# v and the attention values as two 1024-column groups with seven block products

## The chip, the cores and the metric

One core of one Trainium2 chip. The metric is the device time of one execution in microseconds; the kernel before takes 1322.12 us, the median of three runs (1322.08 to 1322.16).

## What is computed

One layer of an encoder on 256 tokens of width 2048, in float32, and a final norm. The parts that the change touches:

```
h = RMSNorm(x);  P = h @ w_in            # columns [u, v | q, k, values | gates]
v = LayerNorm(gelu(v));  y_A = u' * (W_s @ v + b)            # u' = gelu(u), 8 groups
y_B = neighbourhood attention of q, k and the values, 16 heads
m = sigmoid(g_A) * (y_A @ Wb_A) + sigmoid(g_B) * (y_B @ Wb_B)
x = x + m @ w_out;  then a gated convolutional MLP, and the final RMSNorm
```

The scale of the first norm is taken out of the product: the matmuls run on x times the norm's weight, and each row's factor comes in when the product is read.

## The kernel before

Every operand of a product is split into a high part, rounded by ScalarE to the type that TensorE takes in one pass (`whi`, L143), and the rest, a subtraction on VectorE (`wlo`, L144). A product is then three matmuls: high by high, low by high, high by low.

The weights come in **pieces** of 512 KB, numbered through the whole program, in the order in which the groups were planned. `begin(i)` (L168) is what is issued ahead of the matmuls of piece i: loads up to piece i + 4 on SP's queue, roundings up to piece i + 3 (one piece ahead in the first four), and the tasks that were set for i with `at(i, f)`, in the order in which they were set. From piece 5 on the roundings stand ahead of the tasks, before it behind them. Each engine works in the order of issue. Five load buffers and four pairs of rounded buffers turn round: a load waits until VectorE has read the piece five before, a rounding until TensorE has used the piece four before.

Three kinds of group use the pieces. `natural` (L181) takes 512 columns, two 128-row blocks of the weights a piece, the activations held still: 12 matmuls a piece. `stationary` (L185) holds the weights still. `wide` (L260, `run_wide` L324) takes 1024 columns, one 128-row block a piece, 12 matmuls as well. For the tile pairs in `quads` it forms seven block products in place of eight from sums of the tiles: 9 matmuls in the first piece of the pair, 12 in the second. For that VectorE makes sums of the weights three pieces ahead (`weight_sums` L305), which are split two pieces ahead (`weight_sums_split` L314), and sums of the activations (`act_sums` L287, `act_sums_split` L298). The products that belong to several outputs have four banks of their own, which are added up and read after the last pair; with the four of the group that is all eight banks.

x is transposed in eight chunks of two 128-column blocks (`x_chunk` L491: four transposes, two ScalarE and two VectorE operations). Piece 0 begins when x and the first weights are there; chunk c is turned at piece c - 1 and its load stands on SP's queue among those of the weights. The squares of x are summed in pieces 5 to 8 and the norm is made in piece 9 (`x_norm` L1126).

The order of the groups before: v as two natural groups (pieces 0 to 15, evicted by ScalarE with gelu), u as two stationary ones, then values, q and k, gates and branch products in turns (`g_at` L1075), the second halves of the gates as two wide groups (`g_gw` L1086, pairs 1, 3, 5), and from there branch products, w_out, the MLP. The values are copied to window tiles by POOL's queue (L618). The attention of a pair of heads runs as tasks beside the pieces (`attend` L710); the merged values are transposed as tasks two pieces after their group (`turn_m` L852).

## Time and profile before

| | us |
|---|---|
| median of three runs | 1322.12 |
| profiled execution | 1321.89 |
| its span | 1319.9 |
| TensorE busy | 1307.3 |
| VectorE busy | 1030.5 |
| ScalarE busy | 755.0 |

The span is the time from the first to the last instruction of the profiled execution. Busy times overlap. A matmul is shown from its start to a modelled end, so that neighbours overlap too; what one costs is the distance between starts. An operation of VectorE or ScalarE is shown slightly longer than the distance to the next one behind it.

### The profile page before, as it was taken

The numbers are of one execution on the slowest core, as the hardware profiler recorded it, in microseconds if no ns is written. First come the engines' busy times: TensorE is split into PE (matmuls) and PEld (weight loads), VectorE is DVE, ScalarE is ACT, GpSimd is POOL, SyncE is SP. The second block draws the span as 40 slices with busy tenths as digits, with TensorE's granted clock in tenths as the row PEclk, the third lists the DMA queues.
The fourth block names the chain that finished last, engine by engine and source line by source line (L and its number), as shares of the span: only waits on it lengthen the run. The fifth ranks groups of instructions, "written<-read, shape, count | busy, mean of one in ns | idle before, by whom it ended". The sixth has DMA issues, their size and how long they took to land.

```text
span 1319.9 us, 19273 instructions
## 1 busy us (share of the span) xinstructions
PE 1307.3 (99%) x6791; PEld 1115.5 (85%) x6791; DVE 1030.5 (78%) x1561; ACT 755.0 (57%) x1127; POOL 101.6 (8%) x192
## 2 busy tenths in 40 slices
PE   9999999999999999999999999999999999999997
PEld 7888888888887888888888888888888888888885
DVE  6477667767598966996787878787878779999997
ACT  6565566667554644556655556565555556555653
POOL 0241155530000000000000000000000000000000
PEclk9999999999999999999999999999999999999999
DMA  9766775755666666665656665656566657656663
GB/s 317 231 189 183 216 224 165 218 173 155 199 176 208 200 197 221 219 214 162 191 179 195 184 194 181 202 176 204 180 195 187 192 154 229 220 192 206 212 197 122
DMA packets 174800, 259.37 MB, mean 197 GB/s; under 512 B 12920, under 2 KB 124400, under 8 KB 174704
## 3 DMA queue, kind: packets, MB, share of 16 engines
q1 hardware_dynamic: 170416, 250.31, 60.9%
q0 software_dynamic: 3968, 7.30, 2.2%
q8 instruction: 53, 0.87, 0.3%
q10 hardware_dynamic: 320, 0.53, 0.1%
q14 instruction: 43, 0.35, 0.1%
HBM read 253.90 MB, written 2.10 MB: 194 GB/s over the span
## 4 chain that ended last, share of the span: by engine, by line
PE 98%; DVE 1%; DMA 0%; ACT 0%; issue 0%; SPq 0%; ACTq 0%; DVEq 0%
PE bank L196 31%; PE bank L200 16%; PE bank L285 10%; PE bank L283 10%; PE bank L284 10%; PE bank L224 7%; PE bank L226 7%; PE bank L225 7%; PE bank L722 1%; DMA wraw<-in_w_in_dram 0%; PE bank L772 0%; PE bank L598 0%; PE bank L762 0%; PE bank L933 0%; PE bank L496 0%
## 5 line engine op out<-in xcount | busy, mean ns | idle before, releaser
L144 DVE TENSOR_TENSOR wlo<-wraw,whi 128x1024 fp32r<-128x1024 f32 (+1 forms) x471 | 553.6, 1186 | 225.6 <-ACT whi L143 120.9
L143 ACT ACTIVATE whi<-wraw 128x1024 fp32r<-128x1024 f32 (+1 forms) x471 | 475.3, 1022 | 225.9 <-PE bank L225 72.1
L196 PE MATMUL bank<-h,whi 128*128 128x512 f32 x1760 | 425.2, 392 | 0.0
L196 PEld LDWEIGHTS bank<-h,whi 128*128 128x128 f32 x1760 | 322.5, 189 | 61.6
L200 PEld LDWEIGHTS bank<-h,wlo 128*128 128x128 f32 x1760 | 225.9, 191 | 8.8
L200 PE MATMUL bank<-h,wlo 128*128 128x256 f32 x1760 | 228.6, 283 | 0.0
L958 ACT ACTIVATE tc<-ta,ck 128x256 f32<-128x256 f32 x86 | 47.1, 594 | 117.1 <-DVE ta L956 117.1
L224 PE MATMUL bank<-whi,h 128*128 128x512 f32 x256 | 102.4, 400 | 0.6 <-ACT whi L143 0.6
L285 PE MATMUL bank<-wlo,a 128*128 128x512 f32 x260 | 101.6, 391 | 0.2 <-DVE wlo L144 0.2
L283 PE MATMUL bank<-whi,a 128*128 128x512 f32 x260 | 101.3, 390 | 0.0
L284 PE MATMUL bank<-whi,a 128*128 128x512 f32 x260 | 101.3, 390 | 0.0
L225 PE MATMUL bank<-whi,h 128*128 128x512 f32 x256 | 100.1, 391 | 0.3 <-DVE h L475 0.3
L226 PE MATMUL bank<-wlo,h 128*128 128x512 f32 x256 | 100.2, 391 | 0.0
L285 PEld LDWEIGHTS bank<-wlo,a 128*128 128x128 f32 x260 | 48.8, 188 | 11.3 <-DVE wlo L144 1.3
L284 PEld LDWEIGHTS bank<-whi,a 128*128 128x128 f32 x260 | 48.9, 188 | 10.1
L283 PEld LDWEIGHTS bank<-whi,a 128*128 128x128 f32 x260 | 48.8, 188 | 10.1
L224 PEld LDWEIGHTS bank<-whi,h 128*128 128x128 f32 x256 | 48.3, 189 | 10.4 <-ACT whi L143 1.1
L226 PEld LDWEIGHTS bank<-wlo,h 128*128 128x128 f32 x256 | 48.1, 188 | 10.6 <-DVE wlo L144 0.4
L225 PEld LDWEIGHTS bank<-whi,h 128*128 128x128 f32 x256 | 48.2, 188 | 10.1 <-DVE h L475 0.8
L1234 POOL DMA_DIRECT2D gfin<-in_norm_final_dram x4 | 2.2, 548 | 696.8 <-DVE tc L969 577.3
L961 DVE SCALAR_TENSOR_TENSOR tc<-ta,ck,tc 128x255 f32<-128x255 f32 x86 | 41.4, 481 | 14.4 <-ACT tc L958 14.4
L948 ACT ACTIVATE tb<-bank 128x256 f32<-128x256 f32 x86 | 28.3, 385 | 42.5 <-PE bank L196 42.2
(254 smaller groups left out, 1702.4 us busy)
## 6 DMA issues: line engine op xcount, KB each, us to landing
wraw<-in_w_up_dram SPq DMA_DIRECT2D x336, 256.0 KB, 3.4
wraw<-in_w_in_dram SPq DMA_DIRECT2D x111, 512.0 KB, 4.3
wraw<-in_w_down_dram SPq DMA_DIRECT2D x86, 512.0 KB, 4.7
wraw<-in_w_in_dram SPq DMA_DIRECT2D x66, 256.0 KB, 3.5
wraw<-in_w_branch_dram SPq DMA_DIRECT2D x32, 512.0 KB, 3.9
wraw<-in_w_out_dram SPq DMA_DIRECT2D x32, 512.0 KB, 4.4
xs<-in_x_dram SPq DMA_DIRECT2D x8, 256.0 KB, 7.4
vw<-va POOLq DMA_DIRECT2D x32, 64.0 KB, 5.3
```

The lines of the kernel that those rows point to most:

```text
L143: nc.scalar.activation(h[:, k, :m], w[:, k, :m], AF.Copy)
L144: nc.vector.tensor_sub(l[:, k, :m], w[:, k, :m], h[:, k, :m].bitcast(F32))
L196: nc.tensor.matmul(p, h[:, k - k0, b * 128:(b + 1) * 128], acts(k), start=k == 0, stop=k == nk - 1)
L200: nc.tensor.matmul(p[:, :T], l[:, k - k0, b * 128:(b + 1) * 128], acts(k)[:, 0, :], start=False, stop=False)
L224: nc.tensor.matmul(p, xh, h[:, kk, :m], start=st, stop=False)
L225: nc.tensor.matmul(p, xl, h[:, kk, :m], start=False, stop=False)
L226: nc.tensor.matmul(p, xh, l[:, kk, :m], start=False, stop=sp)
L283: nc.tensor.matmul(p, xh, h, start=st, stop=False)
L284: nc.tensor.matmul(p, xl, h, start=False, stop=False)
L285: nc.tensor.matmul(p, xh, l, start=False, stop=sp)
L958: nc.scalar.activation(v, u, AF.Identity, scale=ck[:, 1, ch:ch + 1], bias=ck[:, 3, ch:ch + 1])
L961: nc.vector.scalar_tensor_tensor(v[:, 1:], u[:, :T - 1], ck[:, 0, ch:ch + 1], v[:, 1:], op0=OP.mult, op1=OP.add)
```

## The change

v and the values become two wide groups at the head of the program (pieces 0 to 15 and 16 to 31), u follows, then q and k in turns with the gates and branch products. Pairs 5 and 6 of v (blocks 2 to 5 of x) and pairs 1, 3 and 5 of the values have seven block products; the sums of the activations for blocks 2, 3 and 4, 5 serve both groups. The blocks of x are taken in an order of their own, chunks of x are turned in the order 0, 3, 1, 4, 2, 5, 6, 7 and loaded in that order behind both halves of the first weights. The sums' tiles lie where y lies later; the second pair of v has a room of its own. v is added up in its tile, gelu and its statistics follow later (pieces 17 and 30 on), the squares of x come in pieces 11 to 14 and the norm in 15. The window copies take both halves at once. The gates' pairs move to 2, 4, 6 in the first group, with the sums later. The diff, cut:

```diff
@@ -40,12 +40,18 @@
...
 WAKE = (9, 8)
-GATE_QUADS = (1, 3, 5)
+V_QUADS, V_ORDER = (5, 6), (0, 1, 6, 7, 8, 9, 10, 11, 12, 13, 2, 3, 4, 5, 14, 15)
+VA_QUADS, VA_ORDER = (1, 3, 5), (0, 1, 2, 3, 6, 7, 4, 5, 8, 9, 12, 13, 10, 11, 14, 15)
+X_TURN = ((0, 0), (3, 1), (1, 2), (4, 3), (2, 4), (5, 5), (6, 7), (7, 9))
+X_SUMS = ((1, 3, 4), (2, 5, 6), (6, 21, 22))
+GATE_PAIRS = (2, 4, 6)
+GATE_QUADS = ((2, 4, 6), (1, 3, 5))
+GATE_ORDER = (tuple(range(16)), (0, 1, 4, 5, 2, 3, 8, 9, 6, 7, 12, 13, 10, 11, 14, 15))
 OUT_PAIRS = (3, 5)
...
 TURN_X2 = (13, 1)
-Y_GAP = 192
+Y_GAP = 224
 DOWN_QUADS = ((4, 6, 9, 11, 14, 16, 18), (3, 5, 8, 10, 13, 15, 17))
@@ -111,9 +117,7 @@
...
                 for k in range(kn):
-                    if k:
-                        load_x(256, 256)
-                    nc.sync.dma_start(w[:, k, :cn], src[r0 + k * 128:r0 + (k + 1) * 128, c0:c0 + cn])
+                    nc.sync.dma_start(w[:, k, :cn], src[r0:r0 + 128, c0 + k * step:c0 + k * step + cn])
             elif nb == 1:
@@ -145,6 +149,9 @@
...
                 part(slice(0, units[i]))
+            elif i == 1:
+                part(slice(0, 1))
+                part(slice(1, 2))
             elif i:
@@ -257,11 +260,12 @@
...
-    def wide(src, row0, order, c0, acts, quads, room, done, sums=None):
+    def wide(src, row0, order, c0, acts, quads, room, done, sums=None, odd=None):
         n0 = plan_wide(src, row0, order, c0)
         boxes = {}
-        for q in quads:
+        for n, q in enumerate(quads):
             i = n0 + 2 * q
+            own = odd if odd and n % 2 else room
             whole[i] = whole[i + 1] = None
@@ -271,7 +275,7 @@
...
             at(i - 3, lambda i=i, b=b: weight_sums(i, b, room))
-            at(i - 2, lambda b=b: weight_sums_split(b, room))
+            at(i - 2, lambda b=b, own=own: weight_sums_split(b, own))
         return ("wide", n0, order, acts, quads, boxes, done)
@@ -341,9 +345,8 @@
...
             if q not in quads:
-                for t in range(NT):
-                    for c in range(2):
-                        plain(i, t, c)
+                for t, c in ((0, 0), (0, 1), (1, 0), (1, 1)) if i > 1 else ((0, 0), (1, 0), (0, 1), (1, 1)):
+                    plain(i, t, c)
                 split_t.pop(i)
@@ -497,8 +500,17 @@
...
+    first_rooms = ("t13", "t24", "h13", "h24", "l13", "l24", "s0", "s1", "s2")
+    def first_room(name, dt):
+        return ypool.tile([128, 2, 512], dt, name=f"y{first_rooms.index('t13' if name == 'f' else name)}")
+    def open_y():
+        for k in range(KD // 2):
+            yT.extend(new_pair(ypool, f"y{k}"))
...
@@ -506,35 +518,47 @@
...
-    def ev_vg(j):
...
-                at(i + 2, lambda: gelu_v(ps, i))
...
-                nc.scalar.activation(gm_pool["v"][t][:, j * 512:(j + 1) * 512], ps[t], AF.Gelu_apprx_tanh,
-                                     scale=st1["r"][:, t:t + 1], accum_out=gm_pool["sum"][:, t, j:j + 1])
...
-                at(i + 1, ln_stats)
...
+    def post_sums(P, x, spare):
+        p1, p5, p6, p7 = P
+        (x11, x12), (x21, x22) = x
+        nc.scalar.activation(x11, p1, AF.Copy)
+        nc.vector.tensor_add(spare, p6, x11)
+        nc.vector.tensor_add(x12, p5, spare)
+        nc.vector.tensor_add(x21, p7, spare)
+        nc.vector.tensor_add(x22, p5, x21)
+    def add_sums(ps, x):
+        for t in range(NT):
+            for c in range(2):
+                nc.vector.tensor_add(x[t][c], ps[t][c], x[t][c])
+    def ev_v_sums(P, i):
+        def go():
+            v = gm_pool["v"] = [gm_pool["p"].tile([128, GMW], F32, name=f"vg{t}") for t in range(NT)]
+            gm_pool["v4"] = [[v[t][:, c * 512:(c + 1) * 512] for c in range(2)] for t in range(NT)]
+            post_sums(P, gm_pool["v4"], junk)
+        at(i + 1, go)
+    def ev_v(ps, i):
+        add_sums(ps, gm_pool["v4"])
+        su = gm_pool["sum"] = const.tile([128, NT], F32, name="vsum")
+        def gelu():
+            for t, v in enumerate(gm_pool["v"]):
+                nc.scalar.activation(v, v, AF.Gelu_apprx_tanh, scale=st1["r"][:, t:t + 1], accum_out=su[:, t:t + 1])
+        at(i + 1, gelu)
+        at(30, ln_stats)
...
         i = cur[0]
...
         nm = const.tile([128, NT], F32, name="nmu")
...
         su = gm_pool["sum"]
-        nc.vector.tensor_add(mu, su[:, :, 0], su[:, :, 1])
-        nc.vector.tensor_scalar(nm, mu, -1.0 / GMW, None, op0=OP.mult)
+        nc.vector.tensor_scalar(nm, su, -1.0 / GMW, None, op0=OP.mult)
         box = {}
@@ -605,22 +629,32 @@
...
-    def ev_va(j):
...
+    def ev_va_sums(P, i):
+        def go():
+            va = at_pool["va"] = [first_room(n, F32) for n in ("t13", "t24")]
+            at_pool["va4"] = [[v[:, c] for c in range(2)] for v in va]
+            post_sums(P, at_pool["va4"], junk)
+        at(i + 1, go)
+    def ev_va(ps, i):
+        add_sums(ps, at_pool["va4"])
+        va = at_pool["va"]
+        def scale():
             for t in range(NT):
-                nc.scalar.activation(va[:, t, :], ps[t], AF.Copy, scale=st1["r"][:, t:t + 1])
...
-                    nc.gpsimd.dma_start(at_pool["v"][r * WIN:(r + 1) * WIN, b, j * 512:(j + 1) * 512],
-                                        va[c0:c0 + WIN, r // 2, :])
...
-                at(i + 1 + r // 2, lambda r=r: windows(r))
...
+                nc.scalar.activation(va[t], va[t], AF.Copy, scale=st1["r"][:, t:t + 1])
+        def windows(r):
+            for b in range(NBLK):
+                c0 = (r % 2) * 64 + WIN0[b]
+                nc.gpsimd.dma_start(at_pool["v"][r * WIN:(r + 1) * WIN, b, :],
+                                    va[r // 2][c0:c0 + WIN].rearrange("p a b -> p (a b)"))
+        at(i + 1, scale)
+        for r in range(ROWS):
+            at(i + 2 + r // 2, lambda r=r: windows(r))
+        at(i + 4, open_y)
@@ -802,13 +836,8 @@
...
                 gate_tile(br)
-                p1, p5, p6, p7 = P
-                g11, g12, g21, g22 = (mg["t", br][:, t, c * 512:(c + 1) * 512] for t in range(2) for c in range(2))
-                nc.scalar.activation(g11, p1, AF.Copy)
-                nc.vector.tensor_add(junk, p6, g11)
-                nc.vector.tensor_add(g12, p5, junk)
-                nc.vector.tensor_add(g21, p7, junk)
-                nc.vector.tensor_add(g22, p5, g21)
+                mg["x", br] = [[mg["t", br][:, t, c * 512:(c + 1) * 512] for c in range(2)] for t in range(NT)]
+                post_sums(P, mg["x", br], junk)
@@ -816,10 +845,7 @@
...
             g = mg["t", br]
-            for t in range(NT):
-                for c in range(2):
-                    v = g[:, t, c * 512:(c + 1) * 512]
-                    nc.vector.tensor_add(v, ps[t][c], v)
+            add_sums(ps, mg["x", br])
@@ -1058,11 +1084,18 @@
...
     xt = lambda k: xT[k]
-    g_vg = [natural(w_in2, 0, KD, V0 + j * 512, 512, xt, ev_vg(j)) for j in range(2)]
+    s_room = {}
+    def sums_room(name, dt):
+        return s_room["p"].tile([128, 2, 512], dt, name=name)
+    first_sums = {2 * q: {} for q, _, _ in X_SUMS}
+    g_v = wide(w_in2, 0, V_ORDER, V0, xt, V_QUADS, first_room, (ev_v_sums, ev_v), first_sums,
+               lambda name, dt: s_room["odd"].tile([128, 2, 512], dt, name=name))
+    g_va = wide(w_in2, 0, VA_ORDER, VA0, xt, VA_QUADS, first_room, (ev_va_sums, ev_va), first_sums)
+    for n, (q, i, j) in enumerate(X_SUMS):
+        sum_acts_at(i, j, first_sums[2 * q], lambda q=q: x_pairs[q], first_room, f"s{n}")
     g_u = [stationary(w_in2, 0, KD, U0 + j * 512, 512, 1, 0, xt, ev_u(j)) for j in range(2)]
-    def g_va(j):
-        return natural(w_in2, 0, KD, VA0 + j * 512, 512, xt, ev_va(j))
     def g_qk(j):
@@ -1072,24 +1105,17 @@
...
-    g_at = [g_va(0), g_qk(0), g_va(1), g_qk(1), g_gate(0, 0), g_qk(2), g_gate(1, 0), g_qk(3), g_gate(0, 1),
-            g_gate(1, 1), g_branch(0, 0)]
-    g_m = [g_branch(1, 0), g_branch(0, 1), g_branch(1, 1)]
-    s_room = {}
-    def sums_room(name, dt):
-        if name == "f" and "st" not in s_room:
-            name = "t13"
-        return s_room["p"].tile([128, 2, 512], dt, name=name)
-    x_sums, m_sums = ({2 * q: {} for q in qs} for qs in (GATE_QUADS, OUT_PAIRS))
-    g_gw = [wide(w_in2, 0, range(KD), (GA0, GB0)[br] + 1024, xt, GATE_QUADS, sums_room,
+    g_at = [g_qk(0), g_gate(0, 0), g_qk(1), g_gate(1, 0), g_qk(2), g_gate(0, 1), g_qk(3), g_gate(1, 1),
+            g_branch(0, 0), g_branch(0, 1)]
+    g_m = [g_branch(1, 0), g_branch(1, 1)]
+    x_sums, m_sums = ({2 * q: {} for q in qs} for qs in (GATE_PAIRS, OUT_PAIRS))
+    g_gw = [wide(w_in2, 0, GATE_ORDER[br], (GA0, GB0)[br] + 1024, xt, GATE_QUADS[br], sums_room,
                  (ev_gate_sums(br), ev_gate_wide(br)), x_sums) for br in range(2)]
...
                 (ev_sums(2 * g, sums_room), ev_out(g)), m_sums) for g in range(2)]
-    for n, q in enumerate(GATE_QUADS):
-        i = g_gw[0][1] - 7 + 2 * n
+    for n, q in enumerate(GATE_PAIRS):
+        i = g_gw[0][1] - 3 + 3 * n
         sum_acts_at(i, i + 1, x_sums[2 * q], lambda q=q: x_pairs[q], sums_room, f"s{n}")
@@ -1108,14 +1134,13 @@
...
     preload[0] = [lambda: load_x(0, 256)]
-    for c in range(2, 8):
-        preload[c] = [lambda c=c: load_x(256 * c, 256)]
+    for n, (c, _) in enumerate(X_TURN[1:]):
+        preload[n + 2] = [lambda c=c: load_x(256 * c, 256)]
     at(0, lambda: x_chunk(0))
...
     at(0, lambda: keep_awake(WAKE[1]))
-    midway[0] = lambda: x_chunk(1)
-    for c in range(2, 8):
-        at(c - 1, lambda c=c: x_chunk(c))
+    for c, i in X_TURN[1:]:
+        at(i, lambda c=c: x_chunk(c))
@@ -1130,9 +1155,9 @@
...
     for c in range(4):
-        at(5 + c, lambda c=c: x_stats(c))
-    at(9, x_norm)
-    at(12, lambda: st1.__setitem__("rb", bcast_cols(st1["r"])))
+        at(11 + c, lambda c=c: x_stats(c))
+    at(15, x_norm)
+    at(30, lambda: st1.__setitem__("rb", bcast_cols(st1["r"])))
@@ -1152,24 +1177,29 @@
...
-    at(14, lambda: turn_ws(0))
-    at(15, lambda: turn_ws(1))
+    at(31, lambda: turn_ws(0))
+    at(32, lambda: turn_ws(1))
     preload[13] = [ld for ld, _ in late]
     for n, (_, f) in enumerate(late):
-        at(17 + n // 2, f)
-    for g in g_vg:
+        at(30 + n // 2, f)
+    def open_attn():
+        xin_st.close()
+        A, at_pool["st"] = pool("attn")
+        at_pool["p"] = A
+        at_pool["kl"] = [A.tile([128, T], F32R, name=f"kl{s}") for s in range(2)]
+        for s in range(2):
+            nc.gpsimd.memset(at_pool["kl"][s][(1 - s) * 64:(2 - s) * 64].bitcast(F32), 0.0)
+        at_pool["v"] = A.tile([128, NBLK, NAW], F32, name="vw")
+        bias_start(g_u[1][1] + 2, 0)
+    at(g_u[0][1] + 1, open_attn)
+    s_room["odd"], odd_st = pool("odd")
+    at(g_v[1] + 15, odd_st.close)
+    run_wide(g_v)
+    run_wide(g_va)
+    for g in g_u:
         run_group(g)
-    run_group(g_u[0])
-    xin_st.close()
-    A, A_st = pool("attn")
-    at_pool["p"] = A
-    at_pool["kl"] = [A.tile([128, T], F32R, name=f"kl{s}") for s in range(2)]
-    for s in range(2):
-        nc.gpsimd.memset(at_pool["kl"][s][(1 - s) * 64:(2 - s) * 64].bitcast(F32), 0.0)
-    at_pool["v"] = A.tile([128, NBLK, NAW], F32, name="vw")
-    bias_start(g_u[1][1] + 2, 0)
-    run_group(g_u[1])
     run_group(g_at[0])
@@ -1177,7 +1207,7 @@
...
     assert at_pool["done"] == HEADS // 2
-    A_st.close()
+    at_pool["st"].close()
     open_m(0)
...
     for g in g_m[1:]:
```

## Rows read from the trace of the kernel before

**Rows 1.** The page: span, busy time of each engine, granted clock in 40 slices.

```profile
span 1319.9 us, 19273 instructions
PE 1307.3 (99%) x6791; PEld 1115.5 (85%) x6791; DVE 1030.5 (78%) x1561; ACT 755.0 (57%) x1127; POOL 101.6 (8%) x192
...
PEclk9999999999999999999999999999999999999999
```

**Rows 2.** Waits of TensorE: engine, line, waited for: us in total, times, longest.

```profile
PE bank L283 <- DVE m L473: 0.9, 1, 0.9
PE bank L224 <- ACT whi L143: 0.6, 1, 0.6
PE bank L225 <- DVE h L475: 0.3, 1, 0.3
```

**Rows 3.** Order of time, TensorE, 17 to 39 us: start, us shown, line, tiles, count.

```profile
17.60 0.60 PE L496 MATMUL bank<-ident,xs 128*128 128x128 f32 x4
...
20.79 0.60 PE L496 MATMUL bank<-ident,xs 128*128 128x128 f32 x4
...
30.94 0.39 PE L224 MATMUL bank<-whi,h 128*128 128x512 f32 x1
...
38.42 0.39 PE L224 MATMUL bank<-whi,h 128*128 128x512 f32 x1
```

**Rows 4.** Order of time, TensorE, first two pieces; in brackets what it waited for.

```profile
6.43 0.66 PE L224 MATMUL bank<-whi,h 128*128 128x512 f32 x1
...
8.28 0.51 PE L224 MATMUL bank<-whi,h 128*128 128x512 f32 x1 [0.61 <-ACT whi L143]
...
11.17 0.60 PE L496 MATMUL bank<-ident,xs 128*128 128x128 f32 x4
```

**Rows 5.** Order of time, VectorE, pieces 3 and 6.

```profile
20.05 1.23 DVE L144 TENSOR_TENSOR wlo<-wraw,whi 128x1024 fp32r<-128x1024 f32 x1
...
27.79 0.87 DVE L475 SCALAR_TENSOR_TENSOR h<-bank,gmix,h 128x256 fp32r<-128x256 f32 x2
```

**Rows 6.** Order of time, VectorE, ahead of the first gate group.

```profile
370.15 0.68 DVE L290 TENSOR_TENSOR t<-h 128x512 f32<-128x512 f32 x1
...
371.81 1.22 DVE L144 TENSOR_TENSOR wlo<-wraw,whi 128x1024 fp32r<-128x1024 f32 x1
...
386.45 0.68 DVE L308 TENSOR_TENSOR t<-wraw 128x512 f32<-128x512 f32 x1
...
388.98 1.28 DVE L837 TENSOR_TENSOR g<-bank,g 128x512 f32<-128x512 f32 x2
...
392.51 2.36 DVE L319 TENSOR_TENSOR l<-t,h 128x1024 fp32r<-128x1024 f32 x2
394.78 2.36 DVE L144 TENSOR_TENSOR wlo<-wraw,whi 128x1024 fp32r<-128x1024 f32 x2
```

**Rows 7.** Order of time, ScalarE, pieces 7 to 11.

```profile
29.71 0.63 ACT L1124 ACTIVATE junk<-xs 128x512 f32<-128x512 f32 x1
...
31.09 1.04 ACT L143 ACTIVATE whi<-wraw 128x1024 fp32r<-128x1024 f32 x1
...
33.63 1.06 ACT L143 ACTIVATE whi<-wraw 128x1024 fp32r<-128x1024 f32 x1
...
41.14 1.06 ACT L143 ACTIVATE whi<-wraw 128x1024 fp32r<-128x1024 f32 x1 [1.96 <-DMA wraw<-in_w_in_dram]
```

**Rows 8.** Order of time, VectorE: norm of x, and the end of a gate group.

```profile
38.59 0.15 DVE L1128 TENSOR_REDUCE ss<-xsq 128x2 f32<-128x8 f32 x1
...
40.01 0.16 DVE L453 TENSOR_TENSOR n_r<-n_r,n_s 128x2 f32<-128x2 f32 x1
...
432.47 2.48 DVE L822 TENSOR_TENSOR g<-bank,g 128x512 f32<-128x512 f32 x4
```

**Rows 9.** Window copies: issues with KB each and us to landing; issue times (ns).

```profile
vw<-va POOLq DMA_DIRECT2D x32, 64.0 KB, 5.3
...
L618 POOL DMA_DIRECT2D vw<-va x32: 496/496/523, 128.2 to 184.7; - x32
```

More of the change, by code (lines that the diff above doesn't have):

```diff
@@ L161, in trunk_kernel @@
     cur = [0]
-    midway = {}
     def run_tasks(i):
@@ L243, in run_group @@
             for b in range(nblk):
-                if b == 1 and i in midway:
-                    midway.pop(i)()
                 products(g, ps, i, b, h, l)
@@ L498, in x_chunk @@
         split_pair(p, xT[2 * c:2 * c + 2], gmix[:, 2 * c:2 * c + 2])
-    yT = [ypool.tile([128, 2, T], F32R, name=f"y{k}") for k in range(KD)]
-    ypool.tile([128, Y_GAP // 4], F32, name="gap")
+    yT = []
+    first_rooms = ("t13", "t24", "h13", "h24", "l13", "l24", "s0", "s1", "s2")
[4 more added lines that the diff above has]
+            yT.extend(new_pair(ypool, f"y{k}"))
+        ypool.tile([128, Y_GAP // 4], F32, name="gap")
     groups = []
@@ L507, in trunk_kernel @@
     gm_pool = {}
-    def ev_vg(j):
-        def done(ps, i):
-            if j == 0:
-                at(i + 2, lambda: gelu_v(ps, i))
-            else:
-                gelu_v(ps, i)
-        def gelu_v(ps, i):
-            G = gm_pool["p"]
-            if j == 0:
-                gm_pool["v"] = [G.tile([128, GMW], F32, name=f"vg{t}") for t in range(NT)]
-                gm_pool["sum"] = const.tile([128, NT, 2], F32, name="vsum")
-            for t in range(NT):
-                nc.scalar.activation(gm_pool["v"][t][:, j * 512:(j + 1) * 512], ps[t], AF.Gelu_apprx_tanh,
-                                     scale=st1["r"][:, t:t + 1], accum_out=gm_pool["sum"][:, t, j:j + 1])
-            if j == 1:
-                at(i + 1, ln_stats)
-        return done
+    def post_sums(P, x, spare):
[24 more added lines that the diff above has]
+        at(30, ln_stats)
     def ln_stats():
         i = cur[0]
-        mu = const.tile([128, NT], F32, name="mu")
         nm = const.tile([128, NT], F32, name="nmu")
@@ L818, in done @@
             g = mg["t", br]
-            for t in range(NT):
-                for c in range(2):
-                    v = g[:, t, c * 512:(c + 1) * 512]
-                    nc.vector.tensor_add(v, ps[t][c], v)
+            add_sums(ps, mg["x", br])
             def sigmoid():
```

8 lines of the change are left out of this document (removed).

## The prediction

> **What bounds the kernel now.** I read the page first, then what TensorE waits for, then the order of time of single stretches. The span is 1319.9 us, TensorE is busy 1307.3 us of it and its granted clock is full in every slice [rows 1]. All its waits for another engine inside the kernel come to a few tenths each; the longest is 0.9 us [rows 2]. So the end is set by the number of TensorE instructions, plus every place where TensorE has to stand. The busy column is no price for a matmul: a 512-column one is shown with 0.39 us, but from 30.94 to 38.42 us lie 33 of them, 0.2267 us each [rows 3]. A piece of 12 matmuls is 2.72 us; with the four transposes of an x chunk a piece takes 3.2 us [rows 3], so a chunk costs 0.49. VectorE is busy 78% of the span, but that is an average over stages: where sums for the seven products are made, it works without a gap, and that is where I look for the new limit.
>
> Pieces are counted as in the code: piece p is one step of the schedule, T(p) the time at which TensorE comes to it. After the change 0 to 15 are v, 16 to 31 the attention values, 32 to 47 u. The profiled run took 1321.89 us, 0.23 below the median of 1322.12; I add up against the former and carry the difference over.
>
> **Matmuls removed.** Five tile pairs with seven block products in place of eight, three matmuls each: 15 x 0.2267 = 3.40 us off the path.
>
> **The start.** From the first matmul at 6.43 to the transposes of piece 1 at 11.17 are 4.74 us, where 12 matmuls and one chunk would take 2.72 + 0.49 [rows 3, 4]: 1.53 lost. Most of it is the wait for the second half of the first weights, whose high part comes only just ahead of 8.28 [rows 4]. After the change that load is third in SP's queue instead of fourth, and the first half feeds six matmuls instead of three. I take 1.15 back (all but the short waits of the first three matmuls); the other end is 0, if the load lands no earlier.
>
> **Stall A, piece 6.** The next wait is that of piece 6 for the low part of its x chunk, 0.3 us by the waits view [rows 2] and 0.46 from start to start; it becomes longer. Three chunks (3, 4, 5) are still turned one piece ahead of their use, and VectorE gets two sets of sums of the activations between them. VectorE's queue from the low weights of piece 3 on: these begin 2.45 after the piece's transposes, at T(2) + 2.45 (as 20.05 after 17.60 [rows 3, 5]). Then come, in program order, one rounding of weights for each of pieces 3 to 8 (6 x 1.135; 2.27 for two, start to start [rows 6]), two sets of sums (2 x 1.66 [rows 6]), one low part of a sum (0.60), and of the x chunks 4, 2 and half of 5 five low parts at 0.40 (a pair is shown with 0.87, the second begins before the first is shown as ended [rows 5]): 6.81 + 3.32 + 0.60 + 2.00 = 12.73, with small gaps 13.1. That is T(2) + 15.5. TensorE wants the last of them at its second matmul of piece 6, T(2) + 4 x 3.21 + 0.23 = T(2) + 13.07. The stall is 2.5 us. The sums of piece 5 are registered ahead of its chunk, so chunk 5 stands behind them; they are 1.66 of it.
>
> **Stall B, piece 8.** In piece 7 the queue is: half a rounding (high part ready at T(7) + 0.67, low part 0.60), the weight sums of the first pair (2.53, from 386.45 to 388.98 [rows 6]), the low part of chunk 6 (0.40): ready at T(7) + 4.3. TensorE wants it at T(7) + 3.21 + 0.23. The stall is 0.85. It grows if the sums have to wait for the weights of piece 11, which are rounded from 33.63 in the kernel before [rows 7]; by this reckoning VectorE is ready for them near 32, so up to 1.7 more.
>
> **Stall C, piece 18, where v ends and the values begin.** The second pair's sums read piece 13, whose load lands behind the five loads of row vectors and is waited for until 41.14 [rows 7]. If it lands then, ScalarE has from 43.6 without a break: two roundings of sums (1.9), high parts of pieces 14 to 17 (4 x 0.95), the squares of x, moved here (4 x 1.38, from 29.71 to 31.09 [rows 7]), the copy of the first product (0.6): until 55.5. Behind the copy VectorE has the four adds after the products (2.5, as the four that are shown with 2.48 [rows 8]), half a rounding (0.60), the weight sums of the first value pair (2.53), the norm of x, moved here (1.6, from 38.59 to 40.01 with its last step [rows 8]; ScalarE's root waits in the middle of it and holds the high part of piece 19 back), the four adds at the end of v (2.4) and then the low part of piece 19 (1.14): 10.8, so 66.4. TensorE without B would be at that matmul by 9.4 for piece 0, then 5 x 3.21, 5.24 with A, 3.21, 2.72, 3.21, 2.04, 2.72, 2.04, 5 x 2.72 and 1.13: near 61.4. B and C together are 5.0 us then, however they share it, since the chain hangs on the load. If the load lands two microseconds earlier, VectorE's own queue is the start of the chain and B and C are 3.3. I take 4.7, near the landing that the row shows; the DMA queues carry the same bytes in nearly the same order.
>
> **Gates.** The 0.9 us wait [rows 2] is TensorE waiting for banks that the transposes of the merged values still hold when the products' banks are taken in piece 2 of the first gate group. The pairs move to 2, 4, 6, so the banks are taken two pieces later, and I count it gone: 1.0 us with the gap around it. The other end is 0, as VectorE has the same sums to make, spread over eight pieces rather than six.
>
> **What I cost at nothing.** Squares and norm, moved back, are out of the way in pieces 5 to 9 but not where they go (in C). The transposes of the small weights and row vectors cost TensorE the same in pieces 30 to 32 as before. The statistics of v and its scaling run beside u as before, where no wait of TensorE shows [rows 2]; what covers them are weights rounded three pieces ahead, and without that they cost up to a piece, 2.7 us. On POOL's queue 16 window copies of 128 KB stand where 32 of 64 KB did (5.3 us to landing [rows 9]), issued in pieces 34 and 35, ahead of the bias loads of pieces 42 on. The first y tile lies on the values, so its write in piece 43 waits for those copies: eight pieces, some 22 us, for 16 issues and a landing, 13 us at half a microsecond for an issue [rows 9]. In the attention part the groups change places; the last head's y is used one piece after it is made instead of five, 2.7 us for a copy and a subtraction.
>
> **The sum.** Off: 3.40 + 1.15 + 0.46 + 1.0 = 6.0. On: A 2.5 + B and C 4.7 = 7.2. Net +1.2 us: 1321.89 + 1.2 + 0.23 = 1323.3.
>
> **Rivals.** (1) The stalls are smaller: piece 13 lands early and VectorE and ScalarE keep closer to TensorE at the seam, so that A and B alone remain (3.4): 1322.12 - 6.0 + 3.4 = 1319.5; with A alone 1318.6; with none 1316.1. For it: TensorE hides nearly everything elsewhere. Against: the queue before piece 6 is made of shown durations. (2) Slower: the backlog isn't worked off between the pairs of the values. Each pair brings 2.53 + 2.27 of sums and 1.66 + 0.60 for the third activation sum, beside 1.14 per piece, and two pairs follow each other in four pieces. Every microsecond by which piece 13 lands later is one more at C; it decides from a landing near 42.3, which gives 1324.8, and with the u cover gone or the gates' gain missing 1325 to 1327. (3) The change doesn't do what it says: the 15 matmuls are gone by count, so this can only be the gates' gain or the start's, 1 us each: 1324.4, still no difference. (4) The clock. It is granted full throughout, also in the first slice, after an engine that had done nothing [rows 1], so no row shows a fall; a stall like A or C is longer than any wait that the rows show. If it fell to the lower of its levels for one piece, 12 matmuls would take twice their time: 2.7 us, 1326.0 for one stall and 1328.7 for two. The Trainium skill, "TensorE: Matmul & The Clock Gate", section "What's actually happening", says that the slow level is the default and that activity releases it; by that rule the stalls could bring it back, which the full clock of the first slice here does not bear out.
>
> The same page, section "Wait — 56ns, not 53.3ns?", gives columns over 2.4 GHz plus 2.5 ns for a matmul behind another, 0.2157 us here; the 15 would then be 3.24. The row's 0.2267 decides.
>
> **How the numbers follow.** Forecast with its ends (B and C from 3.3 to 5.2, start and gates from 0 to full) 0.5: 1321.9 to 1326.0. Rival 1: 0.24. Rival 2: 0.17. Rival 3: 0.04. Rival 4: 0.05. A measurement can tell 0.2%, 2.6 us: the bounds are 1319.5 and 1324.8. Most of rival 1 lies below: faster 0.2. Rivals 2 and 4 and the upper end of the forecast: slower 0.27. Same 0.53. The range leaves out about one in ten on either side: 1318.2 to 1326.5.
>
> **What would show it.** In the profile after: TensorE waiting for an x low part at about 26 to 28 us and again near 35, and for a low weight at 62 to 66 with VectorE busy throughout; no wait for a bank in the gates; 6776 matmuls with as many of 512 columns fewer as 15. The forecast is wrong if VectorE shows idle time ahead of those three places, if the norm of x stands elsewhere in its queue, or if waits turn up in u or the attention part.

## The result, and the profile after

The changed kernel takes 1324.49 us (median of 20 runs, 1322.30 to 1326.21) against 1321.98 for the kernel before on the same chip (20 runs): a ratio of 1.0018, 95% interval 1.0011 to 1.0025. By the bound of 0.2% that is no difference, though the interval leaves out 1: the medians differ by 2.5 us where 1.2 was forecast. The time lies 1.2 us above the forecast of 1323.3 and inside its range. (In the experiments below one single run, of the squares alone, took 4652.69 us; its ratio leaves it out.) The profiled run took 1323.59 us, its span 1321.8. What is new is the spread: 0.8 us between all but one run of before, 4 us here.

The page of the changed kernel, span, busy times and granted clock [rows 1]:

```profile
span 1321.8 us, 19329 instructions
PE 1306.0 (99%) x6776; PEld 1112.4 (84%) x6776; DVE 1066.8 (81%) x1625; ACT 765.3 (58%) x1139; POOL 89.5 (7%) x176
...
PEclk9999999999999999999999999999999999999999
```

The 15 matmuls are gone (6791 to 6776). VectorE has 36 us more. The clock's row looks as before; a slice of it is 33 us long, and that hid the most interesting part of the result.

What TensorE waits for now (engine, line, waited for: us in total, times, longest), against [rows 2]:

```profile
PE bank L288 <- DVE h L478: 3.0, 3, 2.3
PE bank L289 <- DVE wlo L148: 1.6, 2, 1.4
PE bank L436 <- POOL ident masks.py:199: 1.4, 1, 1.4
PE bank L287 <- DVE vg L533: 0.3, 1, 0.3
```

The gates' wait for a bank is gone. In its place stand x low parts (`h`, L478: stalls A and B), and low weights and v's adds at the seam (L148, L533: stall C). POOL's 1.4 is the start of the program and was there before.

In order of time, TensorE at piece 6, and then the granted clock of two stretches (the stretch, its us, TensorE's busy us and matmuls, granted clock, share of the DMA engines, GB/s):

```profile
25.44 0.39 PE L287 MATMUL bank<-whi,h 128*128 128x512 f32 x1
28.15 0.50 PE L288 MATMUL bank<-whi,h 128*128 128x512 f32 x1 [2.32 <-DVE h L478]
...
29.59 0.63 PE L287 MATMUL bank<-whi,h 128*128 128x512 f32 x1
30.01 0.63 PE L288 MATMUL bank<-whi,h 128*128 128x512 f32 x1
```

```profile
29.20:32.60 3.40, 3.40 (x11) 0.50 0.87 352
32.60:36.00 3.40, 3.34 (x16) 1.00 0.50 139
```

Stall A is there as forecast: 2.71 us from start to start. A microsecond after it the matmuls stand 0.427 apart, twice the 0.2133 that 512 columns take at 2.4 GHz: the granted clock is 0.50, the lower level, for 3.4 us, and half of that, 1.7 us, is lost. TensorE's busy column calls the stretch full.

Stall B, at piece 8, and the seam, where v ends and the values begin:

```profile
35.55 0.39 PE L287 MATMUL bank<-whi,h 128*128 128x512 f32 x1
36.34 0.50 PE L288 MATMUL bank<-whi,h 128*128 128x512 f32 x1 [0.41 <-DVE h L478]
```

```profile
62.39 0.39 PE L289 MATMUL bank<-wlo,h 128*128 128x512 f32 x1
63.11 0.47 PE L287 MATMUL bank<-whi,h 128*128 128x512 f32 x1 [0.33 <-DVE vg L533]
...
64.11 0.39 PE L288 MATMUL bank<-whi,h 128*128 128x512 f32 x1
65.94 0.50 PE L289 MATMUL bank<-wlo,h 128*128 128x512 f32 x1 [1.44 <-DVE wlo L148]
```

**The sum from the trace.** Distances between starts of TensorE, before against after; a usual distance is 0.23, the first of a piece that turns a chunk 0.32.

| term | forecast | trace |
|---|---|---|
| 15 matmuls (mean distance 0.2288) | -3.40 | -3.43 |
| start: to piece 2's transposes, 14.38 less one chunk (0.49) before, 12.52 after | -1.15 | -1.37 |
| old wait of piece 6 (0.776 - 0.32) | -0.46 | -0.46 |
| gates' bank (1.252 - 0.227) | -1.0 | -1.03 |
| stall A (2.710 - 0.32) | +2.5 | +2.39 |
| clock behind it | none | +1.7 |
| stall B (0.793 - 0.32) and C (0.49 + 1.60) | +4.7 | +2.56 |
| u's first banks (0.19 + 0.37, at 103.5) | 0 | +0.56 |
| sum | +1.2 | +0.9 |

The profiled runs differ by 1.70, their spans by 1.91. The other 0.8 to 1.0 us lie in distances of which none is more than 0.15 above the usual. That the net came out near is luck, as two errors met: B and C cost 2.1 us less, clock and u 2.3 us more.

### The profile page after: what moved, and what is told of

It reads as the page before. It is cut to its first block, busy times and chain, and to the rows that moved or that the text cites. A ratio compares the mean times of both kernels' runs of the same rounds, so it can differ in the third digit from the quotient of the medians.

```text
span 1321.8 us, 19329 instructions
## 1 busy us (share of the span) xinstructions
PE 1306.0 (99%) x6776; PEld 1112.4 (84%) x6776; DVE 1066.8 (81%) x1625; ACT 765.3 (58%) x1139; POOL 89.5 (7%) x176
## 4 chain that ended last, share of the span: by engine, by line
PE 95%; DVE 2%; ACT 1%; issue 1%; DMA 0%; ACTq 0%; SPq 0%; DVEq 0%
PE bank L201 30%; PE bank L205 16%; PE bank L289 11%; PE bank L288 11%; PE bank L287 11%; PE bank L229 4%; PE bank L231 4%; PE bank L230 4%; DVE wlo L148 1%; ACT whi L147 1%; PE bank L756 1%; PE bank L806 0%; PE bank L622 0%; PE bank L796 0%; PE bank L887 0%
## 5 line engine op out<-in xcount | busy, mean ns | idle before, releaser
L148 DVE TENSOR_TENSOR wlo<-wraw,whi 128x1024 fp32r<-128x1024 f32 (+1 forms) x472 | 551.0, 1178 | 192.5 <-ACT whi L147 99.2
L288 PE MATMUL bank<-whi,h 128*128 128x512 f32 x204 | 80.3, 394 | 3.0 <-DVE h L478 3.0
L289 PE MATMUL bank<-wlo,h 128*128 128x512 f32 x204 | 80.5, 395 | 1.4 <-DVE wlo L148 1.4
L287 PE MATMUL bank<-whi,h 128*128 128x512 f32 x204 | 81.0, 397 | 0.3 <-DVE vg L533 0.3
L288 PEld LDWEIGHTS bank<-whi,a 128*128 128x128 f32 x260 | 48.8, 188 | 10.2
L229 PE MATMUL bank<-whi,y 128*128 128x512 f32 x128 | 50.5, 394 | 0.0
L229 PE MATMUL bank<-whi,h 128*128 128x512 f32 x128 | 50.4, 394 | 0.0
L231 PE MATMUL bank<-wlo,h 128*128 128x512 f32 x128 | 49.9, 390 | 0.0
L231 PE MATMUL bank<-wlo,y 128*128 128x512 f32 x128 | 49.9, 390 | 0.0
```

Source lines behind the costliest of these rows:

```text
L148: nc.vector.tensor_sub(l[:, k, :m], w[:, k, :m], h[:, k, :m].bitcast(F32))
L229: nc.tensor.matmul(p, xh, h[:, kk, :m], start=st, stop=False)
L231: nc.tensor.matmul(p, xh, l[:, kk, :m], start=False, stop=sp)
L287: nc.tensor.matmul(p, xh, h, start=st, stop=False)
L288: nc.tensor.matmul(p, xl, h, start=False, stop=False)
L289: nc.tensor.matmul(p, xh, l, start=False, stop=sp)
```

## The experiments

All times are medians; ratios are to the kernel before on the same chip (1322.0 to 1322.2 in every set), with their 95% intervals.

**Chunks ahead of sums, piece by piece.**

```
+    for c, i in X_TURN[1:]:
+        at(i, lambda c=c: x_chunk(c))
     first_sums = {2 * q: {} for q, _, _ in X_SUMS}
...
-    for c, i in X_TURN[1:]:
-        at(i, lambda c=c: x_chunk(c))
```

> The changed kernel with the turning of an x chunk put ahead of the sums of the same piece (pieces 3 to 9); nothing else differs. Theory Q (the price is VectorE's order, and the seam is paced by TensorE: piece 13's weights have landed at 38.33 us but ScalarE begins them at 42.24, when TensorE has left their buffers): chunk 5's low part comes 1.66 us earlier, so the stall at piece 6 falls from 2.5 to about 0.8 us, the one at piece 8 goes (0.57), no stretch at half clock follows (1.8), the seam starts earlier by the same and its 2.1 stay: 1324.5 - 4.0 = about 1320.5 us, and the spread of 4 us between runs shrinks. Rival L (the seam hangs on the load of piece 13, as the prediction had it): its end stays near 65.9 us, the wait there grows to some 6 us, and the time stays within 0.5 us of 1324.5.

1323.88 us, ratio 1.0015 (1.0006 to 1.0024). Stall A fell to 1.12 (a low weight at 20.1 us) and 0.48, the one at piece 8 went; but at the seam TensorE now stands 1.80 and 1.61, in place of 0.49 and 1.60, and the half clock follows there (65.3 to 68.7 us). The copy of the first product, from which the seam's chain starts, moved by 1.0 only, from 54.37 to 53.35. Most of what A and B gave up (1.45) came back at the seam (1.3): theory Q is wrong, and rival L is right only in that the seam's end moves less than TensorE's arrival, 1.0 for 2.3. ScalarE began piece 13's weights 2.7 us earlier, at 39.56, and then waited 1.55 until 42.17 for VectorE's sums of the weights (`y`, L314), so these belong to the chain too. New is a wait at the end of u: at 151 us TensorE waits 0.9 for VectorE (`ya`, L626), as it does for 0.5 and 0.8 us in two of the kernels below; why stays open. Whether the seam hangs on the load, the next run says.

**The row vectors' loads later.**

```
-    preload[13] = [ld for ld, _ in late]
+    preload[20] = [ld for ld, _ in late]
```

> The changed kernel with the five loads of row vectors moved from ahead of piece 13's weights to ahead of piece 20's. Theory Q: piece 13 lands several us earlier, but ScalarE waits for TensorE there, so the seam and the time stay: 1324.5 within 0.5. Rival L: the chain to piece 18 begins up to 3 us earlier and the 2.1 us at the seam go: about 1322.4.

1323.87 us, ratio 1.0011 (1.0002 to 1.0020). The seam's waits are the same to the hundredth (0.49 and 1.60) and so is stall A. Not the load, then: in the changed kernel, ScalarE begins piece 13's weights at 42.24, as soon as TensorE has left their buffer, and piece 13 is there by then.

**Keeping TensorE at work during stall A.**

```
+    at(6, lambda: keep_awake(18))
```

> The changed kernel with 18 more transposes of the identity (0.11 us each, some 2 us of work whose result nobody reads) ahead of piece 6's matmuls, where TensorE would stand for 2.5 us; the wait for the x low part stays where it is. Theory K (the clock falls because TensorE does nothing there): no stretch of 0.427 us per matmul between 29 and 33 us, the time falls by about 1.8 to 1322.7 and the spread between runs shrinks. Rival M (the fall belongs to the place, or to something other than TensorE's standing still): the stretch stays, the time is 1324.5 or a little more.

1323.48 us, ratio 1.0011 (1.0002 to 1.0020), runs from 1322.20 to 1325.24. Granted clock in two stretches:

```profile
28.00:32.00 4.00, 3.66 (x19) 1.00 0.95 363
...
64.00:68.00 4.00, 3.07 (x7) 0.63 0.45 131
```

The wait for the x low part is over at 28.4 us, much as before, and the clock behind it stays full. That fits theory K and does not show it: in three profiles further down (squares and norm in front, the squares alone, one pair less) the clock stays full behind the same stand without any transposes. The median fell by 1.0 in place of 1.8, and in the profiled run, 1324.50, the 3.4 us at half clock turned up behind the seam instead, after 0.48 and 1.61 us of waiting.

**Squares and norm of x back in pieces 5 to 9.**

```
-        at(11 + c, lambda c=c: x_stats(c))
-    at(15, x_norm)
+        at(5 + c, lambda c=c: x_stats(c))
+    at(9, x_norm)
```

> The changed kernel with the squares and the norm of x where the kernel before has them (squares in pieces 5 to 8, norm in piece 9). Theory S (squares on ScalarE and norm on VectorE are what makes the seam late): ScalarE, idle for some 8 us between 24 and 36, takes the squares there; its chain ahead of the first product's copy is 5.5 us shorter and VectorE has 1.6 less ahead of piece 19's low weights; the two waits at 62 to 66 us (2.1 together) go: about 1322.4. Rival V (VectorE's sums alone make the seam late): at least 1 us of the 2.1 stays, or the stall at piece 6 grows by as much as the seam loses: 1323.5 to 1325.

1320.49 us, ratio 0.9988 (0.9979 to 0.9997). Both waits of the seam are gone, stall A is as long as ever (2.50 over the usual), B 0.87. More was won than the 2.1 of the seam, because this profile has no half clock either; the medians differ by 4.0, and what the clock did in the runs without a profile is not known.

**The squares alone.**

```
-        at(11 + c, lambda c=c: x_stats(c))
+        at(5 + c, lambda c=c: x_stats(c))
```

> The changed kernel with the squares of x alone back in pieces 5 to 8; the norm stays in piece 15, behind the weight sums of the first value pair. If ScalarE's chain of squares ahead of the first product's copy makes the seam late (theory S1): the two waits at 62 to 66 us go as in e_stats, 1320.5 within 0.5. If the norm's place in VectorE's queue, and ScalarE's root behind it, makes it late (theory S2): most of the 2.1 us stays, 1322.5 or more.

1320.71 us, ratio 0.9991 (0.9982 to 1.0000): theory S1. The norm, which the prediction put in the chain with 1.6 us and a ScalarE root that holds up the next weights, holds up nothing once the squares are gone. What it costs beside the squares was not tried; in the changed kernel it stands in VectorE's queue from 60.77 to 62.28, between the copy and v's adds. ScalarE in order of time in the changed kernel, from piece 13's weights to the copy, with one of four pairs of squares:

```profile
42.24 1.06 ACT L147 ACTIVATE whi<-wraw 128x1024 fp32r<-128x1024 f32 x1 [1.75 <-issue]
43.20 1.99 ACT L322 ACTIVATE h<-y 128x1024 fp32r<-128x1024 f32 x2
45.10 1.05 ACT L147 ACTIVATE whi<-wraw 128x1024 fp32r<-128x1024 f32 x1
46.05 0.62 ACT L1149 ACTIVATE junk<-xs 128x512 f32<-128x512 f32 x1
...
54.37 0.58 ACT L524 ACTIVATE vg<-bank 128x512 f32<-128x512 f32 x1
```

and the same copy with the squares back in front:

```profile
48.67 0.58 ACT L524 ACTIVATE vg<-bank 128x512 f32<-128x512 f32 x1
```

From 42.20 to 55.00 ScalarE is busy 12.64 of 12.8 us; from 24 to 36 it had been busy 4.5 of 12. The squares, 5.5 us, had been moved out of an idle stretch into the one stretch where ScalarE sets the pace.

**One seven-product pair of v less** (with squares and norm in front).

```
-V_QUADS, V_ORDER = (5, 6), ...
+V_QUADS, V_ORDER = (6,), ...
...
-X_SUMS = ((1, 3, 4), (2, 5, 6), (6, 21, 22))
+X_SUMS = ((2, 5, 6), (1, 12, 13), (6, 21, 22))
```

> The changed kernel with squares and norm back in pieces 5 to 9 (as in e_stats, 1320.5 us) and one of the two seven-product pairs of v taken out: three matmuls more (0.68 us), VectorE without 4.8 us of weight sums and their low parts and with the first activation sums (2.3) in pieces 12 and 13 instead of 3 and 4. Theory V (VectorE works without a gap from piece 3 to the seam; what it has to do by then sets the time, wherever the stalls stand): stalls at pieces 6 and 8 (2.5 + 0.87) go, nothing comes back at the seam: about 1317.8. Rival Q (the stalls are single places of bad order, and each pair pays for itself): the time rises by the 0.68: 1321.2, or falls by no more than 1.

1320.59 us, ratio 0.9991 (0.9982 to 1.0000), the same as with both pairs (1320.49). Theory V fell: with 2.3 us less for VectorE ahead of piece 6 and 4.8 less behind it, stall A did not change (2.54). B went, 0.37 came at the seam, and the three matmuls more cost the rest. VectorE from the low parts of chunk 2 to the one that ends the stall (the second of the last row), in this kernel:

```profile
20.55 0.88 DVE L478 SCALAR_TENSOR_TENSOR h<-bank,gmix,h 128x256 fp32r<-128x256 f32 x2 [1.04 <-ACT h L471]
21.50 4.63 DVE L148 TENSOR_TENSOR wlo<-wraw,whi 128x1024 fp32r<-128x1024 f32 x4
26.04 0.69 DVE L294 TENSOR_TENSOR y<-h 128x512 f32<-128x512 f32 x1
...
27.70 0.87 DVE L478 SCALAR_TENSOR_TENSOR h<-bank,gmix,h 128x256 fp32r<-128x256 f32 x2
```

The sums taken away had filled VectorE's gaps, here 1.04 us ahead of a chunk. What makes the stall begins at 20.4, when ScalarE has rounded chunk 2, turned in piece 4: the schedule asks for one piece of weights ahead up to piece 3 and for three from piece 4 on, so pieces 4 and 5 ask for the low parts of four pieces in a row (4.63), then come the second sums (1.66), and chunk 5 behind both.

**The sums of the activations on GpSimd** (with squares and norm in front).

```
-        nc.vector.tensor_add(f, a[:, :, 0, :].bitcast(F32), a[:, :, 1, :].bitcast(F32))
+        nc.gpsimd.tensor_add(f, a[:, :, 0, :].bitcast(F32), a[:, :, 1, :].bitcast(F32))
...
```

> The changed kernel with squares and norm back in pieces 5 to 9 (as in e_stats, 1320.5 us) and the sums of the activations (two sets in pieces 3 and 5, one in 21; 1.66 us each on VectorE) made by GpSimd, which does nothing there. The matmuls stay. Theory V (VectorE's amount of work by the seam sets the time): 3.3 us less ahead of piece 6, so that the stall there falls from 2.5 to 0, the one at piece 8 (0.87) stays or goes, the seam stays without a wait: 1317.2 to 1318.0. Rival G (GpSimd's sums come late or hold VectorE up, or the stalls have another cause): less than 1 us gained, 1319.5 or more.

1324.24 us, ratio 1.0013 (1.0004 to 1.0022): rival G, and 3.7 us worse than without the edit. VectorE's low parts of the weights beside GpSimd's second set (line, tiles, count, busy and mean ns):

```profile
L148 DVE TENSOR_TENSOR wlo<-wraw,whi 128x1024 fp32r<-128x1024 f32 x4 | 6.3, 1622 | 0.1
```

and without it, in the changed kernel:

```profile
L148 DVE TENSOR_TENSOR wlo<-wraw,whi 128x1024 fp32r<-128x1024 f32 x4 | 4.6, 1220 | 0.1
```

The four low parts take 1.6 us more and GpSimd needs 5.2 and 7.0 us for a set in place of 1.66, so nothing came free ahead of piece 6: stall A is 2.81, and 0.7 and 0.76 of new waits and 3.4 us at half clock behind A (1.7) come to it. The Trainium skill, "SBUF — State Buffer", section "SBUF: two separate sides", says that a VectorE operation with two inputs in SBUF and a GpSimd operation that reads SBUF hold one pair of ports in turn, each for its whole length; these rows agree in that both engines' operations got longer (1.22 to 1.62 us; GpSimd's 128 x 128 adds and subtractions from 0.46 to 1.33 and more beside VectorE's low parts).

**The gates' edit alone, in the kernel before.**

```
-GATE_QUADS = (1, 3, 5)
+GATE_PAIRS = (2, 4, 6)
+GATE_QUADS = ((2, 4, 6), (1, 3, 5))
+GATE_ORDER = (tuple(range(16)), (0, 1, 4, 5, 2, 3, 8, 9, ...))
...
-        i = g_gw[0][1] - 7 + 2 * n
+        i = g_gw[0][1] - 3 + 3 * n
```

> The kernel before with the change's edit of the gates alone: first gate group with its pairs at 2, 4, 6, the second with its order turned round, activation sums three pieces apart, a room of their own for the first step of the sums. As predicted (the wait for banks of 0.9 us, 1.0 with its gap, goes): 1321.0. The rival (the wait is hidden elsewhere or turns into another): within 0.3 of 1322.0.

1320.75 us, ratio 0.9989 (0.9980 to 0.9998), 1.3 us less than before; the wait of [rows 2] is gone and no other has come in the gates. This term was right.

**Waits put into the kernel before**, for the clock alone.

```
+    def stand(k):
+        p = bank()
+        nc.tensor.transpose(p[:, :128], ident, ident)
+        nc.scalar.activation(slow, p[:, :128], AF.Copy)
+        for _ in range(k):
+            nc.scalar.activation(slow, slow, AF.Copy)
+        nc.tensor.transpose(p[:, :128], slow, ident)
...
+    for n in range(24):
+        at(g_up[0][1] + 8 + 6 * n, lambda k=(1, 3, 5, 7, 9, 12, 16)[n % 7]: stand(k))
```

> The kernel before with 24 waits put into the up stage, one each six pieces: TensorE turns a tile, ScalarE copies it and then copies it over itself 1 to 16 times, and TensorE turns the copy, so that TensorE stands for some 0.7 to 5 us; nobody reads the result. Theory K (after TensorE has stood for a few us the clock may be taken back): stretches with 0.427 us per matmul follow the longer stands, none follows the shorter, and whether one follows a stand of some 2.5 us differs from stand to stand, as the runs of the changed kernel differ. Rival M (the clock falls only at the place of the x chunks): the granted clock stays full. The sum of the stands, some 50 us, is added to the time; only the clock behind them matters.

1485.07 us, one run. The 24 stands took from 1.65 to 8.9 us, 117 us together where some 50 were expected. Two of them, and the granted clock from a stand's start to the next one's, for these two, one of the longest and the shortest:

```profile
628.38 0.27 PE L1124 MATMUL bank<-ident 128*128 128x128 f32 x1
630.71 0.33 PE L1128 MATMUL bank<-ident,slow 128*128 128x128 f32 x1 [2.05 <-ACT slow L1127]
793.90 0.27 PE L1124 MATMUL bank<-ident 128*128 128x128 f32 x1
797.38 0.33 PE L1128 MATMUL bank<-ident,slow 128*128 128x128 f32 x1 [3.21 <-ACT slow L1127]
```

```profile
628.38:649.66 21.28, 19.23 (x103) 0.92 0.43 134
...
793.90:814.29 20.39, 17.18 (x101) 1.00 0.50 156
...
1073.70:1100.25 26.55, 19.58 (x101) 0.81 0.39 119
...
1127.22:1145.74 18.52, 17.15 (x100) 1.00 0.55 171
```

At 22 stands the clock fell. It stayed full at the shortest (1.65) and at one of 3.5 us, while one of 2.3 had 3.4 us at half clock behind it. At the longer stands the fall comes while TensorE still stands: at 1073.70, a stand of 7.2, the clock is at half for 10.2 us, 5.0 of them inside the stand, where they cost nothing, and 5.2 behind it. Behind the 22 stands lie from 2.8 to 6.1 us at half clock. So theory K is shown by these stands, in another part of the program, and rival M is wrong; with one correction: between 2.3 and 3.5 us the length does not decide.

**Every chunk turned earlier, and the squares in front.**

```
-X_TURN = ((0, 0), (3, 1), (1, 2), (4, 3), (2, 4), (5, 5), (6, 7), (7, 9))
-X_SUMS = ((1, 3, 4), (2, 5, 6), (6, 21, 22))
+X_TURN = ((0, 0), (3, 1), (2, 2), (4, 2), (1, 3), (5, 3), (6, 5), (7, 6))
+X_SUMS = ((2, 3, 4), (1, 4, 5), (6, 21, 22))
...
-        at(11 + c, lambda c=c: x_stats(c))
-    at(15, x_norm)
+        at(4 + c, lambda c=c: x_stats(c))
+    at(9, x_norm)
```

> The changed kernel with squares in pieces 4 to 7 and the norm in piece 9, and every x chunk turned at least two pieces ahead of its use (chunks 0, 3, 2, 4, 1, 5, 6, 7 in pieces 0, 1, 2, 2, 3, 3, 5, 6; sums of the activations of chunk 2 in pieces 3 and 4, of chunk 1 in 4 and 5). Theory B (the stall at piece 6 is the low part of chunk 5 behind the four roundings that pieces 4 and 5 ask for at once, 4.6 us on VectorE, and the sums): no wait over 0.6 us is left in v, some 1.5 us of small ones; against e_stats the 2.5 and 0.87 go and 1.5 come: 1318.9, or 1318.3 where no stand is left that the clock falls after; the spread between runs shrinks to that of the kernel before. Rival V (VectorE's amount of work by the seam is the bound): the waits come back between 60 and 66 us, 1320 or more.

1318.37 us, ratio 0.9973 (0.9963 to 0.9984), runs from 1317.94 to 1319.15: the fastest of all, 3.7 us under the kernel before. TensorE's waits for VectorE inside it:

```profile
PE bank L289 <- DVE wlo L148: 0.9, 3, 0.6
```

Theory B: with chunks 2 and 5 turned well ahead of the four low parts, stall A is gone, and with the squares out of the chain nothing comes back at the seam but 0.35.

**The same order of chunks, squares and norm left late.**

```
-X_TURN = ((0, 0), (3, 1), (1, 2), (4, 3), (2, 4), (5, 5), (6, 7), (7, 9))
-X_SUMS = ((1, 3, 4), (2, 5, 6), (6, 21, 22))
+X_TURN = ((0, 0), (3, 1), (2, 2), (4, 2), (1, 3), (5, 3), (6, 5), (7, 6))
+X_SUMS = ((2, 3, 4), (1, 4, 5), (6, 21, 22))
```

> The changed kernel with the order of the chunks and activation sums of e_turn; squares and norm of x stay in pieces 11 to 15 as the change has them. If the stalls are separate (theory Q): those at pieces 6 and 8 go (2.5 + 0.6, and 1.8 of half clock), 1.5 of small waits come, the 2.1 at the seam stay: 1321.1. If they share one bound (theory C: ScalarE's chain from piece 13's weights, landed at 38.33 us, over six pieces of high parts and sums with the squares between them, to the first product's copy): the copy moves forward by less than 2 us, TensorE arrives 4 us earlier and waits the rest there: seam waits of 4 us or more, 1322.8 to 1323.8.

1322.15 us, ratio 0.9998 (0.9989 to 1.0007), between the two expectations. In the profiled run, the longest of the eleven (1323.89), the seam's waits grew to 1.79 and 1.60, with the clock down behind them; the copy came at 52.44, 1.9 earlier. That is the mechanism of theory C with 3.4 us of waiting for the 4 expected. Here piece 13's weights were waited for:

```profile
39.94 1.06 ACT L147 ACTIVATE whi<-wraw 128x1024 fp32r<-128x1024 f32 x1 [2.77 <-DMA wraw<-in_w_in_dram]
```

So the load is the next bound, 2.3 us ahead of the one that held in the changed kernel.

**The changed kernel once more.**

> The changed kernel once more, nothing altered, for a second profile of it. Theory K (whether the clock falls after a stand, and which, is not fixed by the program): the same stalls within 0.2 us (2.5 at piece 6, 2.1 at the seam), but another sum of half clock (none, or 3.4 or 6.8 us of it, after piece 6 or after the seam), and the time differs from the 1323.59 of the first profile by the half of that difference. Rival: the same stretch after piece 6 again, the same time within 0.3.

1322.91 us. Stall A and the seam are the same (2.48 and 2.11 over the usual), the half clock again behind A, 0.5 us later; stall B is gone, 0.57. So the place was the same as in the first profile, as the rival said, and theory K's differing sum was not seen. The time is 0.68 us shorter, of which B is 0.57; the rival had 0.3.

## Why the prediction was right, and where it was not

**Right by mechanism and size:** the matmuls, the start, the old wait, the gates (in the trace and by themselves), and stall A at 2.5 us with the x low part of piece 6 behind the sums. The working of A was nearly right for the wrong reason: it added up VectorE's queue from the low weights of piece 3, without gaps. So it is in the changed kernel, but with 2.3 us of that work taken away the stall stayed; what decides are the low parts of four pieces in a row and one set of sums, behind ScalarE's work on chunk 2.

**Stalls B and C: one term mis-sized, 4.7 for 2.6.** The step that failed took the landing of piece 13's weights from the row of before (41.14 [rows 7]) as the start of the chain, a fixed time. SP issued that load 1.8 us earlier in the changed kernel (33.01 for 34.81), and the chain began when TensorE freed the buffer, at 42.24: it follows TensorE. That it still ran near the times reckoned (ScalarE at the second pair's sums at 43.2 for 43.6, the last low part at 65.9 for 66.4) is luck, for by then the half clock had held TensorE back by 1.7. Where the clock stayed full behind A, in the run with the transposes, TensorE came to the seam 1.0 earlier, the chain began 1.0 earlier (41.23), and the waits were 0.48 and 1.61 again. The chain itself, ScalarE's with the four squares and VectorE's adds and sums behind the copy, was named correctly; the norm's share of it was not measured by itself.

**The sum of A and C.** The prediction treated A as a cost beside B and C. They are tied: twice, with A and B eased, the seam's waits grew by 1.3 us, because the copy of the first product moved by only 1.0 (ScalarE waited for VectorE's weight sums) and 1.9 (it waited for the load). The table's terms can be added, but not taken away one by one.

**Rival 4, the clock, came true once, at 1.7 us, with a chance of 0.05.** Two readings failed. First, "also in the first slice" rested on [rows 1], whose slices average 33 us and whose clock is shown as full until its first recorded change. The spacing tells otherwise: the four transposes of the first chunk are shown with 1.11 us, those of the next with 0.60.

```profile
3.96 1.11 PE L496 MATMUL bank<-ident,xs 128*128 128x128 f32 x4 [0.18 <-DMA xs<-in_x_dram]
...
9.34 0.60 PE L496 MATMUL bank<-ident,xs 128*128 128x128 f32 x4
```

These are of the kernel before: TensorE starts at the lower level there too, with transposes 0.213 us apart, 0.109 later. So the page of the Trainium skill that the prediction set aside, "TensorE: Matmul & The Clock Gate", section "What's actually happening", was borne out: slow is the default, and activity releases it. Second, the longest wait of before, 0.9 us, says nothing of a stand of 2.3.

**u, costed at nothing,** cost 0.56. The cover that the prediction named, weights rounded ahead, held. What it did not look for is a bank: u's first products want those of the values, which are free only after the four adds of the wide form (L533). No wait is named there; it is read from the order of time, in which the first two adds end at 103.87 and 104.46 and the products that were late start at 103.92 and 104.52.

**Its own signs.** Of the signs that the prediction gave for being wrong two turned up: VectorE stood idle for 2.45 us ahead of stall B, until ScalarE had its high part ready (32.67), and a wait turned up in u. And ahead of the seam's copy it was ScalarE that worked without a gap (12.64 of 12.8 us); VectorE was busy 10.03 of them.

**The spread** of 4 us was not forecast. The squares' kernel has the same stall A to the hundredth as the changed one, 25.44 to 28.15, and the clock behind it is full:

```profile
28.15 0.50 PE L288 MATMUL bank<-whi,h 128*128 128x512 f32 x1 [2.32 <-DVE h L478]
...
29.18 0.40 PE L289 MATMUL bank<-wlo,h 128*128 128x512 f32 x1
29.42 0.39 PE L287 MATMUL bank<-whi,h 128*128 128x512 f32 x1
```

```profile
29.20:32.60 3.40, 3.40 (x18) 1.00 0.85 340
```

So equal stands are answered differently. Seven profiles have a stand of 2.5 to 2.8 us there: in the four in which the clock's first rise is recorded at 5.1 to 5.9 us (the changed kernel twice, the later loads, GpSimd) it fell behind the stand, in the three with the rise at 6.2 to 7.0 (squares and norm, the squares alone, one pair less) it did not. The run with the transposes has its rise at 7.0 too. So what the clock does is not settled by the stand alone. None, one or two falls of 1.7 us would give the spread; where no stand is left it is 1.2 us, but with GpSimd's sums, where a stand of 2.8 is left, it is 0.9. That the runs of the changed kernel differ for this reason is argued, not shown: its two profiles have one fall each.

**Still open:** whether the transposes had any part in the full clock behind stall A; what the norm costs beside the squares; why the median of the changed kernel is 0.9 us above its profiled run; and how much of the 0.8 us that the table leaves over is one thing.

## What to carry to other kernels

A step that costs nothing where an engine idles can delay what stands behind it by its full length in the stretch where that engine leads (here 5.5 us of squares, and the copy 5.7 us later): before moving it, look at the busy time of both stretches. Ask of each stall on which chain its end hangs; stalls on one chain share one price, and the cure is to take out the longest part of the chain that need not stand there. Add up a stand of TensorE like those here (2.3 us and more) with the half clock that may follow it, and read that clock in short windows and in the distance of equal matmuls, not in a page's digits.

## What the runs showed of the hardware

After a stand of TensorE the clock sometimes falls to 1.2 GHz and sometimes does not, with the same stand at the same place. Of 24 stands put in, the clock fell at 22; it did not at 1.65 and at 3.5 us, the shortest with a fall was 2.3. It fell at the seam after waits of 0.48 and 1.61 us in one run and stayed full after the same waits in others. The fall is recorded anywhere from 6.6 us before the end of a stand to 1.5 us after it, and lasts 3.4 to 10.2 us; matmuls then stand 0.427 us apart per 512 columns though TensorE is fully at work. At the start of the program TensorE is at 1.2 GHz as well; the first rise is recorded at 5.1 to 7.3 us. A VectorE subtraction of 128 x 1024 elements took 1.62 us on average beside GpSimd's adds and 1.22 without; GpSimd's add of 128 x 512 took 2.1 to 2.3 us where VectorE's took 0.68.
